# Interleaved steps of a hybrid attention and state-space block, set in the middle of projection units

## The chip, the cores and the metric

The kernel runs on one core of one Trainium2 chip. The metric is device microseconds per execution; the time shown is the median of three runs. The engines are TensorE (PE in the profile, with its weight loads as PEld), VectorE (DVE), ScalarE (ACT), GpSimd (POOL) and SyncE (SP), which issues the transfers.

## What is computed

One layer of a decoder trunk on 512 tokens of width 1024, in fp32: RMSNorm, one combined input projection, three branches that read it (A: banded attention over a window of 128 with sinks, B: dilated attention, C: a diagonal state-space model), each projected, gated and summed, an output projection, then a gated conv-FFN and a last RMSNorm. Cut to what the change touches:

```python
def banded_attention(q, k, v, max_offset, sink=None):   # 4 blocks of 128 queries
    ...                                                  # a block sees its own keys and the block before
    s = jnp.where(mask[None, :, None, None], s, NEG_INF)
    m = jnp.maximum(jnp.max(s, axis=-1, keepdims=True), sk)
    p = jnp.exp(s - m)
    l = jnp.sum(p, axis=-1, keepdims=True) + jnp.exp(sk - m)
    o = jnp.einsum("nbgrqk,nbkgd->nbgrqd", p, vv) / l

def s5_mixer(u, ...):                                    # 32 groups, 64 complex states each
    bu_re = jnp.einsum("bsgh,gph->bsgp", uf, bb_re)
    ...
    _, _, xr, xi = lax.associative_scan(combine, (a_re, a_im, bu_re, bu_im), axis=1)
    y = Re(C x) + D u

def hybrid_mixer(h, w_in, ...):
    proj = h @ w_in                                      # 1024 -> 5632 columns
    qa, ka, va, qd, kd, vd, u, g = jnp.split(proj, cuts, axis=-1)
    ...
```

## The kernel before

**Products.** fp32 products are made of three matmuls in a rounded format (fp32r): every weight is split into a high part `whi` and a low part `wlo`, the activations h likewise into `hTh` and `hTl`. `mm3` (L171 to L173) issues high by high, high by low, low by high. A weight chunk is loaded by SyncE into one of two `raw` buffers; `Chunk.split` then makes `whi` on ScalarE (L66) and `wlo` on VectorE (L92), or on VectorE (L91) and GpSimd in the start.

**Units.** The projections are a list of units. One unit makes 128 columns of the projection for all 512 tokens: `tile_mm` loops over 8 blocks of the contraction and issues three matmuls for each, 24 in all, into a PSUM bank of the tag "mm". ScalarE evicts it (`pj`, or `th` for a gate). Units 1 to 6 make q, k and v of branch A, 7 to 14 its gates, 15 to 24 q, k and v of branch B.

**Steps between units.** `run` goes through the units. For unit u it first splits a piece of the next chunk, then runs the functions that the table `plan` has for u (filled by `before(u, ...)`, L1347 ff.), then the unit itself. All engines take their instructions in the order in which this program issues them (a manual schedule), so the table is the order. The steps are:

- `attn_a(i)`, i = 0 to 3: branch A, block i, a generator of five stages (four for i = 0, which has one block of keys). Step 1: half of the scores into two "sc" banks (L764), maxima by VectorE (L771). Step 2: the other half, and then the whole softmax: maxima, `nmA`, `esA`, ScalarE's eight exponentials with sums (L780), `lA`, its reciprocal (L782), eight products (L269). Step 3: transposes of the probabilities into the "pt" banks (L794), copied to `pTA` by ScalarE. Steps 4 and 5: products with V into an "o" bank (L800), and for i > 0 the second block of keys.
- `ssm_m1(j)`, j = 0 to 3: 32 matmuls into two "sc" banks (L684), four products `z` by VectorE from these banks, sums by GpSimd, two scans by VectorE (L694, L695), then the products that make the states `X`, with differences by GpSimd.
- `ssm_m2(j)`: state to output, matmuls L718 and L720 into an "o" bank, four copies to `yS`, in turns ScalarE and VectorE (L725).
- `ssm_e(j)`: tables for `ssm_m1(j)`, on GpSimd. `ssm_ob(j)`: output matrices. `to_nat`: transposes of V.

**The start.** x is scaled by its norm in pieces (`scale1`: L363 for piece 0, L366 for piece 1), transposed by TensorE (`nt`, L340), converted to `hTh` and `hTl`, and the products for the state-space input u come first (`u_first`, L388).

Of the kernel before, what the change touches and what calls it, by code (L numbers as in the profile page):

```python
# [20 lines left out]
KD = DM // 128  # L21
# [10 lines left out]
def hybrid_block(  # L32
# [19 lines left out]
    def slot(shape, dt=F32, name="s"):  # L52
        return sl.tile(shape, dt, tag="s", name=name)
# [142 lines left out]

    def before(u, *fns):
        plan.setdefault(u, []).extend(fns)

    def run(first, live):  # L200
        order, start, last = [], [], {}
        for u, (c, _) in enumerate(units):
            if id(c) not in last:
                order.append(c)
                start.append(u)
            last[id(c)] = u
        state = {"loaded": 1, "live": live}
        done = [0] * len(order)
        done[0] = len(first.defs)

        def load_to(n):
            while state["loaded"] < min(n, len(order)):
                order[state["loaded"]].load()
                state["loaded"] += 1

        def split_to(ci, n):
            if ci >= len(order):
                return
            c = order[ci]
# [12 lines left out]
        for u, (c, fn) in enumerate(units):
            ci = order.index(c)
            cur = max(cur, ci)
            split_to(ci, 99)
            assert done[ci] == len(c.defs)
            fs = plan.get(u, []) + later
            later.clear()
            if u in AUX_FIRST:
                for f in fs:  # L240
                    f()
                fs = []
            if cur + 1 < len(order):
                left = len(order[cur + 1].defs) - done[cur + 1]
                split_to(cur + 1, done[cur + 1] - (-left // (start[cur + 1] - u)))
            for c2, n in early.get(u, []):
                split_to(order.index(c2), n)
            for f in fs:
                f()
            fn()  # L250
            if last[id(c)] == u and not c.own:
                state["live"] -= len(c.defs)

# [95 lines left out]
    vcol = cst([128, 8], "vcol")  # L349
# [7 lines left out]
    def rstd1(t):  # L357
        rstd_of(stat[:, 4 + t:5 + t], stat[:, t:t + 1])

    def scale1(t):  # L360
        xv, rs = xa[t // 2][:, t % 2, :], stat[:, 4 + t:5 + t]
        if t % 2 == 0:
            V.tensor_scalar(xv, xv, rs, None, op0=ALU.mult)  # L363
        else:
            copy_act(xv[:, 512:], xv[:, 512:], scale=rs)
            V.tensor_scalar(xv[:, :512], xv[:, :512], rs, None, op0=ALU.mult)  # L366
# [13 lines left out]
    def u_first(c):  # L380
        for a in range(2):
            ups[c, a] = bank("mm" if c == 0 else "o")
        half = KD // 2
        for kind, ks in ((0, range(KD)), (2, range(half)), (1, range(KD)), (2, range(half, KD))):
            for a in range(2):
                for k in ks:
                    w, xa_ = cu[c].get(k, a)[kind // 2], h_act(k)[kind % 2]
                    PE.matmul(ups[c, a][:, P0_], w, xa_[:, P0_], start=kind == 0 and k == 0,  # L388
                              stop=kind == 2 and k == KD - 1)
# [237 lines left out]
    def ssm_inj(j):  # L627
        bd = BDs[j % 2]
        INJ[j] = [slot([128, 4, 128], name="inj") for _ in range(2)]
        for i in range(2):  # L630
            pb = bank("pt")
            for t in range(4):
                PE.transpose(pb[:, t * 128:(t + 1) * 128],
                             bd[i][:, t].rearrange("p k g h -> p (k g h)"), ident)
            copy_act(INJ[j][i][:, :, :], pb[:, :].rearrange("p (t c) -> p t c", t=4))
        pk = bank("o", (128, 4, 32))
        for t in range(4):
            for i in range(2):
                PE.matmul(pk[:, t, :], bd[i][:, t].rearrange("p k g h -> p (k g h)"),
                          V0b[i][:, 4 * t + j].rearrange("p g h -> p (g h)"), start=(i == 0), stop=(i == 1))  # L640
        tz = TZ[j]
        for ti in range(4):
            for to in range(ti + 1, 4):
                b = 3 - (to - ti)
                copy_act(tz[32 * ti:32 * ti + 32, :, to, :], pk[32 * b:32 * b + 32, :, :])
        for ti in range(4):
            tt(tz[32 * ti:32 * ti + 32, :, ti, :], pk[96:128, :, :],
               DI[0][96:128].rearrange("p (t j) c -> p t j c", j=4)[:, :, j, :], ADD)
# [28 lines left out]
    def ssm_m1(j):  # L677
        Er, Ei = Es.pop(j)
        s = []
        inj = INJ.pop(j)  # L680
        for i in range(2):
            pb = bank("sc", (128, 4, 128))
            for t in range(4):
                PE.matmul(pb[:, t, :], inj[i][:, t, :], US[j][:, t, :], start=True, stop=True)  # L684
            s.append(pb[:, :, :].rearrange("p t c -> p (t c)"))
        a, b, zr, zi = (slot([128, 512], name="z")[:, :] for _ in range(4))
        tt(zr, s[0], Er, MUL)
        tt(a, s[1], Ei, MUL)
        tt(zi, s[1], Er, MUL)
        tt(b, s[0], Ei, MUL)  # L690
        tt(zr, zr, a, ADD, G)
        tt(zi, zi, b, SUB, G)
        a4 = A4s.pop(j)[:, :, :].rearrange("p t c -> p (t c)")
        V.tensor_tensor_scan(a, a4, zr, 0.0, op0=MUL, op1=ADD)  # L694
        V.tensor_tensor_scan(b, a4, zi, 0.0, op0=MUL, op1=ADD)  # L695
        X = [slot([128, 4, 128], name="X") for _ in range(2)]
        x3 = slot([128, 512], name="xt")[:, :]

        def sh(v):
            return v.rearrange("p (t c) -> p t c", c=128)[:, :, 0:127]  # L700

        for i in range(2):
            G.memset(X[i][:, :, 0:1], 0.0)
        tt(zr, a, Er, MUL)
        tt(x3, b, Ei, MUL)
        tt(X[0][:, :, 1:128], sh(zr), sh(x3), SUB, G)
        tt(zi, a, Ei, MUL)
        tt(b, b, Er, MUL)
        tt(X[1][:, :, 1:128], sh(zi), sh(b), ADD, G)
        Xs[j] = X  # L710

    def ssm_m2(j):
        if not yS:
# [26 lines left out]
    proj = {}  # L740
# [602 lines left out]
    def st_(g):  # L1343
        return lambda: next(g)
# [8 lines left out]
    before(4, lambda: ssm_inj(0), lambda: ssm_bd(1), lambda: ssm_e(0), st_(CP))  # L1353
    before(5, lambda: ssm_inj(1), lambda: ssm_bd(2))
    before(6, lambda: ssm_inj(2), lambda: ssm_bd(3), st_(CP))
    before(7, lambda: ssm_inj(3), st_(A[0]))
    before(8, lambda: VA.append(to_nat(proj["vA"], "VA")), lambda: ssm_ob(0), st_(A[0]))
    before(9, lambda: ssm_m1(0), lambda: ssm_ob(1), lambda: ssm_e(1))
    before(10, lambda: ssm_ob(2), st_(A[0]), st_(A[1]))
    before(11, lambda: ssm_ob(3), st_(A[0]), st_(A[1]))  # L1360
    before(12, lambda: ssm_m2(0), lambda: ssm_m1(1), lambda: ssm_e(2))
    before(13, st_(A[1]), st_(A[2]))
    before(14, st_(A[1]), st_(A[2]))
    before(15, st_(A[1]), lambda: ssm_m2(1), lambda: ssm_m1(2), lambda: ssm_e(3))
    before(16, st_(A[2]), st_(A[3]))
    before(17, st_(A[2]), st_(A[3]))
    before(18, st_(A[2]), lambda: ssm_m2(2), lambda: ssm_m1(3))
    before(19, st_(A[3]))
    before(20, st_(A[3]), lambda: VB.setdefault(0, [to_nat(proj["vB", 0], "VB0")]))
    before(21, st_(A[3]), lambda: VB[0].append(to_nat(proj["vB", 0], "VB1", True)), lambda: ssm_m2(3))  # L1370
    before(22, lambda: VB.setdefault(1, [to_nat(proj["vB", 1], "VB0")]))
    before(23, lambda: VB[1].append(to_nat(proj["vB", 1], "VB1", True)))
    for u, h in ((25, 0), (26, 0), (28, 0), (30, 0), (31, 1), (32, 1), (33, 0), (34, 1), (35, 0), (36, 0), (36, 1),
                 (37, 0), (38, 0), (39, 1), (41, 1), (42, 1), (43, 1), (44, 1)):
        before(u, st_(B[h]))
# [40 lines left out]
```

## Time and profile before

| what | value |
|---|---|
| median of three runs | 839.84 us (839.41 to 841.44) |
| the profiled execution | 840.54 us, of which 838.7 us span |
| TensorE busy | 814.7 us, 97% of the span |
| VectorE busy | 479.3 us, 57% |
| ScalarE busy | 353.8 us, 42% |
| GpSimd busy | 168.2 us, 20% |
| granted TensorE clock, mean | 0.994 of full speed |

Busy is the time in which an engine works on an instruction of its own; a matmul that waits inside a group of several is partly counted as busy. The rest of the 840.54 us lies around the span. A row of the waits says which instruction of an engine waited and which one released it.

### The profile page before, as it was taken

Reading aid. Unit: us, or ns where it says so; the run is one execution under the profiler, and the core shown is the slowest. Engines: PE = TensorE matmul, PEld = TensorE weight load, DVE = VectorE, ACT = ScalarE, POOL = GpSimd, SP = SyncE. Lnnn points to the kernel's source line nnn. Section 1 sums busy time; section 2 is a strip of 40 time slices with the busy share of each in tenths; the row PEclk is TensorE's granted clock in tenths of the full one; section 3 lists DMA queues with packets and bytes.
Section 4 is the critical chain, followed back from the end, with each engine's and each line's share of the span. In section 5 each row is a group of like instructions: output and inputs, shape, how many; then the busy total and the mean of one; then the engine's idle time right before and its main releaser. Section 6 shows DMA issues by size and latency. Waiting matters only on the chain.

```text
span 838.7 us, 10519 instructions
## 1 busy us (share of the span) xinstructions
PE 814.7 (97%) x4085; PEld 676.3 (81%) x4085; DVE 479.3 (57%) x921; ACT 353.8 (42%) x665; POOL 168.2 (20%) x217
## 2 busy tenths in 40 slices
PE   7999899989999999999999999999999999999996
PEld 7988768667777888888878998888888888888885
DVE  7898397697335637363655456556655555422313
ACT  5546453535435555352444344444444443313212
POOL 6199752562100100013530000000000000002002
PEclk9999999999999999999999999999999999999999
DMA  9333111111243113232362313333333323422402
GB/s 243 98 102 101 40 61 52 51 51 51 50 106 102 52 51 102 68 102 82 101 227 74 101 52 100 101 101 100 101 101 101 100 77 101 150 63 89 151 0 101
DMA packets 68278, 76.60 MB, mean 91 GB/s; under 512 B 8161, under 2 KB 55557, under 8 KB 68229
## 3 DMA queue, kind: packets, MB, share of 16 engines
q1 hardware_dynamic: 67972, 75.89, 28.4%
q8 instruction: 32, 0.52, 0.3%
q0 software_dynamic: 256, 0.05, 0.1%
q14 instruction: 18, 0.14, 0.1%
HBM read 73.81 MB, written 2.12 MB: 91 GB/s over the span
## 4 chain that ended last, share of the span: by engine, by line
PE 82%; DVE 9%; ACT 2%; issue 2%; POOL 2%; DMA 1%; SPq 0%; POOLq 0%; DVEq 0%; ACTq 0%
PE up L172 10%; PE up L173 10%; PE up L171 10%; PE mm L171 9%; PE mm L173 9%; PE mm L172 9%; PE acc L178 6%; PE acc L179 6%; PE acc L177 6%; DVE wlo L92 1%; DMA x<-in_x_dram 1%; DVE z L279 1%; PE sc L896 1%; PE nt L340 1%; POOL th L279 1%
## 5 line engine op out<-in xcount | busy, mean ns | idle before, releaser
L92 DVE TENSOR_TENSOR wlo<-raw,whi 128x1024 fp32r<-128x1024 f32 (+1 forms) x126 | 154.2, 1232 | 149.6 <-ACT whi L66 149.4
L66 ACT ACTIVATE whi<-raw 128x1024 fp32r<-128x1024 f32 (+1 forms) x126 | 127.4, 1024 | 58.4 <-PE acc L179 56.2
L171 PE MATMUL up<-hTh,whi 128*128 128x512 f32 (+1 forms) x384 | 142.9, 372 | 0.0
L172 PE MATMUL up<-hTl,whi 128*128 128x512 f32 (+1 forms) x384 | 142.8, 372 | 0.0
L173 PE MATMUL up<-hTh,wlo 128*128 128x512 f32 (+1 forms) x384 | 142.8, 372 | 0.0
L171 PE MATMUL mm<-hTh,whi 128*128 128x512 f32 (+1 forms) x336 | 132.3, 394 | 0.0
L173 PE MATMUL mm<-hTh,wlo 128*128 128x512 f32 (+1 forms) x336 | 129.5, 385 | 0.0
L172 PE MATMUL mm<-hTl,whi 128*128 128x512 f32 (+1 forms) x336 | 129.4, 385 | 0.0
L275 DVE SCALAR_TENSOR_TENSOR cc<-up,cpar,cc 128x511 f32<-128x511 f32 x88 | 66.0, 749 | 97.3 <-ACT cc L1108 95.7
L171 PEld LDWEIGHTS up<-hTh,whi 128*128 128x128 f32 x384 | 72.4, 189 | 12.5
L172 PEld LDWEIGHTS up<-hTl,whi 128*128 128x128 f32 x384 | 72.4, 189 | 12.4
L173 PEld LDWEIGHTS up<-hTh,wlo 128*128 128x128 f32 x384 | 72.4, 189 | 12.4
L171 PEld LDWEIGHTS mm<-hTh,whi 128*128 128x128 f32 x336 | 63.3, 188 | 14.5 <-issue 2.5
L173 PEld LDWEIGHTS mm<-hTh,wlo 128*128 128x128 f32 x336 | 63.2, 188 | 12.8
L172 PEld LDWEIGHTS mm<-hTl,whi 128*128 128x128 f32 x336 | 63.3, 188 | 11.5
L178 PE MATMUL acc<-wlo,gh 128*128 128x512 f32 x172 | 67.0, 390 | 0.0
L179 PE MATMUL acc<-whi,gl 128*128 128x512 f32 x172 | 67.0, 389 | 0.0
L177 PE MATMUL acc<-whi,gh 128*128 128x512 f32 x172 | 67.0, 389 | 0.0
L279 POOL TENSOR_TENSOR x<-x,gfin 128x512 f32<-128x512 f32 x4 | 5.2, 1289 | 296.8 <-ACT acc L1047 296.8
L1108 ACT ACTIVATE cc<-up,cpar 128x512 f32<-128x512 f32 x44 | 34.3, 779 | 61.2 <-PE up L173 60.5
L990 ACT ACTIVATE th<-mm 128x512 f32<-128x512 f32 x24 | 14.3, 594 | 71.1 <-PE mm L173 58.2
L66 ACT ACTIVATE gh<-cc 128x512 fp32r<-128x512 f32 x22 | 13.9, 632 | 59.4 <-DVE cc L279 59.4
(298 smaller groups left out, 1278.9 us busy)
## 6 DMA issues: line engine op xcount, KB each, us to landing
raw<-in_w_up_dram SPq DMA_DIRECT2D x22, 1024.0 KB, 5.0
raw<-in_w_in_dram SPq DMA_DIRECT2D x18, 1024.0 KB, 5.1
raw<-in_w_down_dram SPq DMA_DIRECT2D x10, 1024.0 KB, 5.0
x<-in_x_dram SPq DMA_DIRECT2D x8, 512.0 KB, 5.9
raw<-in_w_in_dram SPq DMA_DIRECT2D x8, 512.0 KB, 5.0
raw<-in_w_out_dram SPq DMA_DIRECT2D x4, 1024.0 KB, 5.1
raw<-in_w_branch_a_dram SPq DMA_DIRECT2D x4, 512.0 KB, 6.2
raw<-in_w_branch_c_dram SPq DMA_DIRECT2D x2, 1024.0 KB, 4.9
```

Of the source, the lines that this page charges most:

```text
L66: S.activation(o, i, AF.Copy)
L92: (lo_eng or V).tensor_tensor(view(lo), r, view(hi).bitcast(F32), op=ALU.subtract)
L171: PE.matmul(ps, wh, xh, start=first, stop=False)
L172: PE.matmul(ps, wh, xl, start=False, stop=False)
L173: PE.matmul(ps, wl, xh, start=False, stop=last)
L177: PE.matmul(ps, xh, wh, start=first, stop=False)
L178: PE.matmul(ps, xh, wl, start=False, stop=False)
L179: PE.matmul(ps, xl, wh, start=False, stop=last)
L275: emit(lambda: V.scalar_tensor_tensor(o, a, s, b, op0=op0, op1=op1))
L279: emit(lambda: (eng or V).tensor_tensor(o, a, b, op=op))
L990: S.activation(t, ps, AF.Tanh, scale=0.5)
L1108: S.activation(dst, ps, AF.Identity, bias=cpar[:, 3, f:f + 1], scale=cpar[:, 2, f:f + 1])
```

## The change

Four things are changed; what is computed stays.

1. `tile_mm` calls the functions in the list `midq` when half of its blocks are done, that is behind 12 of the 24 matmuls. `mid(u, ...)` puts functions there for unit u.
2. `ssm_m1` becomes a generator with two stages: up to the scans, and the rest.
3. The table of steps of units 7 to 24 is written anew, with `mid` for most of the scores and state-space steps.
4. In the start, `scale1(1)` and the copy of `vcol` come ahead of the split of the first weight piece.

```diff
     def tile_mm(ps, w, c, nk, act, o=slice(0, T)):
 
         for k in range(nk):
+            if k == nk // 2:
+                for f in midq:
+                    f()
+                midq.clear()
             xh, xl = act(k)
...
+            midq.extend(mids.get(u, []))
             fn()
...
         V.tensor_tensor_scan(a, a4, zr, 0.0, op0=MUL, op1=ADD)
         V.tensor_tensor_scan(b, a4, zi, 0.0, op0=MUL, op1=ADD)
+        yield
         X = [slot([128, 4, 128], name="X") for _ in range(2)]
...
     rstd1(1)
+    V.tensor_copy(vcol, pv[:, 0:8])
+    scale1(1)
     cu[0].split(0, V, G)
-    scale1(1)
-    V.tensor_copy(vcol, pv[:, 0:8])
     cu[0].split(1, V, G)
...
-    before(11, lambda: ssm_ob(3), st_(A[0]), st_(A[1]))
-    before(12, lambda: ssm_m2(0), lambda: ssm_m1(1), lambda: ssm_e(2))
-    before(13, st_(A[1]), st_(A[2]))
...
+    before(11, lambda: ssm_ob(3), st_(A[0]))
+    mid(11, st_(A[1]))
+    before(11, lambda: ssm_e(1))
+    before(12, lambda: ssm_m2(0))
+    mid(12, st_(A[1]))
+    before(13, st_(A[1]))
+    mid(13, st_(M[1]))
```

The whole table, with the unit at which each step is issued ("m" is the middle of the unit; A are the steps 1 to 5 of a block, M the two stages of `ssm_m1`, which before is one step):

| step | before | after |
|---|---|---|
| block 0: 1, 2, 3, 4 | 7, 8, 10, 11 | 7m, 8m, 10, 11 |
| block 1: 1 to 5 | 10, 11, 13, 14, 15 | 11m, 12m, 13, 14, 15 |
| block 2: 1 to 5 | 13, 14, 16, 17, 18 | 15m, 16m, 17, 18, 19 |
| block 3: 1 to 5 | 16, 17, 19, 20, 21 | 19m, 20m, 21, 22, 23 |
| `ssm_m1(0)` to `(3)` | 9, 12, 15, 18 | 9m 10m, 13m 14m, 17m 18m, 21m 22m |
| `ssm_m2(0)` to `(3)` | 12, 15, 18, 21 | 12, 15, 19, 24 |
| `ssm_e(1)`, `(2)`, `(3)` | 9, 12, 15 | 11, 16, 20m |

**TensorE between step 2 and step 3 of block 1.** Before, the scores stand at the start of unit 11 (its 24 matmuls are those of mm_1549), then come `ssm_m2(0)` (o_1583), the matmuls of `ssm_m1(1)`, all of unit 12 (mm_1645) and the transposes of the probabilities smA:

```order
L764 MATMUL sc_1516<-pj_1114,pj_933 128x256
L764 MATMUL sc_1517<-pj_1114,pj_933 128x256
...
L764 MATMUL sc_1517<-pj_1114,pj_1041 128x256
L171 MATMUL mm_1549<-hTh_125,whi_1354 128x512
...
L173 MATMUL mm_1549<-hTh_125,wlo_1435 128x512
L718 MATMUL o_1583<-us_903,tz_156 128x128
...
L684 MATMUL sc_1600<-us_978,inj_1047 128x128 x4
L684 MATMUL sc_1605<-us_978,inj_1048 128x128 x4
L171 MATMUL mm_1645<-hTh_125,whi_1354 128x512
...
L794 MATMUL pt_1677<-ident_83,smA_1471 128x128 x2
L794 MATMUL pt_1677<-ident_83,smA_1522 128x128 x2
```

Now they stand in the middle of unit 12, whose matmuls go to mm_1567:

```order
L777 MATMUL sc_1580<-pj_1114,pj_933 128x256
L777 MATMUL sc_1581<-pj_1114,pj_933 128x256
...
L777 MATMUL sc_1581<-pj_1114,pj_1041 128x256
L171 MATMUL mm_1567<-hTh_125,whi_1411 128x512
...
L173 MATMUL mm_1567<-hTh_125,wlo_1412 128x512
L807 MATMUL pt_1632<-ident_83,smA_1523 128x128 x2
L807 MATMUL pt_1632<-ident_83,smA_1586 128x128 x2
L807 MATMUL pt_1639<-ident_83,smA_1526 128x128 x2
```

The same scores and the same transposes, with 12 matmuls of a unit between them in place of 48 matmuls and two state-space steps.

**VectorE around the same softmax.** Before, the maxima (L771), sums and products of block 1, with the copies of yS behind them:

```order
L279 TENSOR_TENSOR ya1_1445<-o_1446,ya0_1444 128x4x128
L771 ISA smA_1522,mxA1_1461<-sc_1516,maskA_131 128x256
...
L771 ISA smA_1525,mxA1_1461<-sc_1517,maskA_131 128x256
L771 ISA mxA1_1461 128x1
L275 SCALAR_TENSOR_TENSOR nmA1_1462<-mxA1_1461,nsink_134 128x8
L279 TENSOR_TENSOR esA1_1464<-sink_123,nmA1_1462 128x8
L279 TENSOR_TENSOR lA1_1463<-lA1_1463,esA1_1464 128x8
L782 RECIPROCAL lA1_1463<-lA1_1463 128x8
L269 TENSOR_SCALAR smA_1471<-smA_1471,lA1_1463 128x256 x2
...
L725 COPY yS_1582<-o_1583 32x512 x2
L279 TENSOR_TENSOR z_1612<-sc_1600,E_1395 128x512
```

After:

```order
L92 TENSOR_TENSOR wlo_1544<-raw_1281,whi_1543 128x1024
L738 COPY yS_1549<-o_1550 32x512 x2
L784 ISA smA_1586,mxA1_1513<-sc_1580,maskA_131 128x256
...
L784 ISA smA_1589,mxA1_1513<-sc_1581,maskA_131 128x256
L784 ISA mxA1_1513 128x1
L286 SCALAR_TENSOR_TENSOR nmA1_1514<-mxA1_1513,nsink_134 128x8
L290 TENSOR_TENSOR esA1_1516<-sink_123,nmA1_1514 128x8
L290 TENSOR_TENSOR lA1_1515<-lA1_1515,esA1_1516 128x8
L795 RECIPROCAL lA1_1515<-lA1_1515 128x8
L280 TENSOR_SCALAR smA_1523<-smA_1523,lA1_1515 128x256 x2
...
L92 TENSOR_TENSOR wlo_1628<-raw_1415,whi_1627 128x1024
L290 TENSOR_TENSOR z_1671<-sc_1659,E_1488 128x512
```

The weight subtraction and the two copies of yS now stand ahead of the second four maxima; the next weight subtraction stands behind the products, as before, and the products z of `ssm_m1(1)` behind that.

**VectorE in the start.** Before:

```order
L330 TENSOR_SCALAR stat_127<-stat_127 128x1
L363 TENSOR_SCALAR x0_88<-x0_88,stat_127 128x1024
L330 TENSOR_SCALAR stat_127<-stat_127 128x1
L91 CAST whi_248<-raw_94 128x1024
L366 TENSOR_SCALAR x0_88<-x0_88,stat_127 128x512
L1257 COPY vcol_128<-o_237 128x8
L91 CAST whi_255<-raw_94 128x1024
```

After:

```order
L341 TENSOR_SCALAR stat_127<-stat_127 128x1
L374 TENSOR_SCALAR x0_88<-x0_88,stat_127 128x1024
L341 TENSOR_SCALAR stat_127<-stat_127 128x1
L1268 COPY vcol_128<-o_237 128x8
L377 TENSOR_SCALAR x0_88<-x0_88,stat_127 128x512
L91 CAST whi_251<-raw_94 128x1024
L91 CAST whi_255<-raw_94 128x1024
```

The scaling of the second half of x (L366, now L377) is ahead of the cast of the weight piece.

## Rows read from the trace of the kernel before

**Rows 1.** What TensorE waits for: line, releaser: us in total, times, longest.

```profile
PE nt L340 <- DVE x L366: 3.4, 1, 3.4
PE sc L684 <- DVE mxA L771: 3.3, 1, 3.3
PE sc L764 <- DVE mxA L771: 3.0, 2, 1.6
PE o L800 <- ACT pTA L66: 2.2, 2, 1.8
PE sc L764 <- DVE z L279: 2.1, 2, 1.6
```

**Rows 2.** TensorE's timeline: start, us, engine, line, operation, operands, [idle before <-releaser].

```profile
101.58 3.40 PE L684 MATMUL sc<-us,inj 128*128 128x128 f32 x16 [3.27 <-DVE mxA L771]
...
131.75 1.95 PE L684 MATMUL sc<-us,inj 128*128 128x128 f32 x16
...
183.43 1.82 PE L764 MATMUL sc<-pj 64*128 64x256 f32 x8 [1.45 <-DVE mxA L771]
...
152.16 1.14 PE L764 MATMUL sc<-pj 64*128 64x256 f32 x8
...
149.64 1.56 PE L800 MATMUL o<-pTA,VA 128*64 128x512 f32 x4 [1.80 <-ACT pTA L66]
...
158.93 1.08 PE L800 MATMUL o<-pTA,VA 128*64 128x512 f32 x4
```

**Rows 3.** Windows: busy us of PE, PEld, DVE, ACT, POOL, granted clock, DMA share, GB/s.

```profile
12.20:15.60 3.40, 3.40 (x18) 3.36 (x17) 2.99 (x8) 3.40 (x10) 2.02 (x1) 0.51 1.35 211
...
101.30:104.30 3.00, 2.71 (x12) 2.72 (x13) 0.99 (x10) 2.51 (x12) 0.00 (x0) 0.50 0.65 207
```

**Rows 4.** Timeline of the start: TensorE, VectorE and GpSimd.

```profile
13.23 3.32 PE L388 MATMUL mm<-hTh,whi 128*128 128x256 f32 x16
...
17.34 2.08 PE L388 MATMUL mm<-hTl,whi 128*128 128x256 f32 x16
...
8.46 2.63 DVE L366 TENSOR_SCALAR x<-x,stat 128x512 f32<-128x512 f32 x1
...
18.42 0.49 DVE L366 TENSOR_SCALAR x<-x,stat 128x512 f32<-128x512 f32 x1 [0.67 <-POOL stat L331]
...
7.53 0.90 POOL L331 TENSOR_TENSOR stat<-stat,mhalf 128x1 f32<-128x1 f32 x1 [0.93 <-DVE stat L330]
8.47 2.34 POOL L92 TENSOR_TENSOR wlo<-raw,whi 128x1024 fp32r<-128x1024 f32 x1
```

**Rows 5.** TensorE's timeline: the first and the last matmul of one unit (24 in all).

```profile
153.22 0.50 PE L171 MATMUL mm<-hTh,whi 128*128 128x512 f32 x1
...
158.61 0.39 PE L173 MATMUL mm<-hTh,wlo 128*128 128x512 f32 x1
```

**Rows 6.** The softmax of block 1, two rows of block 0's, and transposes that don't wait.

```profile
124.55 0.41 DVE L771 CUSTOM_DVE_ANT_0 smA<-sc,maskA 128x256 f32<-128x256 f32 x1
...
125.57 0.41 DVE L771 CUSTOM_DVE_ANT_0 smA<-sc,maskA 128x256 f32<-128x256 f32 x1
...
127.39 0.49 ACT L780 ACTIVATE smA<-smA,nmA 128x256 f32<-128x256 f32 x1
...
131.89 2.19 DVE L269 TENSOR_SCALAR smA<-smA,lA 128x256 f32<-128x256 f32 x8
...
101.66 0.29 DVE L771 CUSTOM_DVE_ANT_0 smA<-sc,maskA 128x128 f32<-128x128 f32 x1
...
102.50 0.39 ACT L780 ACTIVATE smA<-smA,nmA 128x128 f32<-128x128 f32 x1
...
151.13 1.09 PE L794 MATMUL pt<-ident,smA 128*128 128x128 f32 x8
```

**Rows 7.** A copy of yS on VectorE; the first exponential of block 3 on ScalarE.

```profile
135.25 1.05 DVE L725 COPY yS<-o 32x512 f32<-32x512 f32 x1
...
189.06 0.49 ACT L780 ACTIVATE smA<-smA,nmA 128x256 f32<-128x256 f32 x1
```

More of the change, by code (lines that the diff above doesn't have):

```diff
@@ L191, in hybrid_block @@
     plan = {}
+    mids = {}
+    midq = []
     def add(chunk, fn):
@@ L198, in before, with mid @@
         plan.setdefault(u, []).extend(fns)
+    def mid(u, *fns):
+        mids.setdefault(u, []).extend(fns)
     def run(first, live):
@@ L249, in run @@
                 f()
+            midq.extend(mids.get(u, []))
             fn()
+            assert not midq
             if last[id(c)] == u and not c.own:
@@ L382, in u_first @@
             ups[c, a] = bank("mm" if c == 0 else "o")
-        half = KD // 2
-        for kind, ks in ((0, range(KD)), (2, range(half)), (1, range(KD)), (2, range(half, KD))):
+        kh = KD // 2
+        for kind, ks in ((0, range(KD)), (2, range(kh)), (1, range(KD)), (2, range(kh, KD))):
             for a in range(2):
@@ L710, in ssm_m1 @@
         Xs[j] = X
+        yield
     def ssm_m2(j):
@@ L1355, in hybrid_block @@
     before(6, lambda: ssm_inj(2), lambda: ssm_bd(3), st_(CP))
[L1356 to L1359, printed above, removed]
-    before(11, lambda: ssm_ob(3), st_(A[0]), st_(A[1]))
-    before(12, lambda: ssm_m2(0), lambda: ssm_m1(1), lambda: ssm_e(2))
-    before(13, st_(A[1]), st_(A[2]))
-    before(14, st_(A[1]), st_(A[2]))
@@ L1364, in hybrid_block @@
[L1364 to L1371, printed above, removed]
@@ L1372, in hybrid_block @@
-    before(23, lambda: VB[1].append(to_nat(proj["vB", 1], "VB1", True)))
+    M = [ssm_m1(j) for j in range(4)]
+    before(7, lambda: ssm_inj(3))
+    mid(7, st_(A[0]))
+    before(8, lambda: VA.append(to_nat(proj["vA"], "VA")), lambda: ssm_ob(0))
+    mid(8, st_(A[0]))
+    before(9, lambda: ssm_ob(1))
+    mid(9, st_(M[0]))
+    before(10, lambda: ssm_ob(2), st_(A[0]))
+    mid(10, st_(M[0]))
+    before(11, lambda: ssm_ob(3), st_(A[0]))
+    mid(11, st_(A[1]))
+    before(11, lambda: ssm_e(1))
@@ new lines, in hybrid_block @@
+    before(12, lambda: ssm_m2(0))
+    mid(12, st_(A[1]))
+    before(13, st_(A[1]))
+    mid(13, st_(M[1]))
+    before(14, st_(A[1]))
+    mid(14, st_(M[1]))
+    before(15, st_(A[1]), lambda: ssm_m2(1))
+    mid(15, st_(A[2]))
+    before(16, lambda: ssm_e(2))
+    mid(16, st_(A[2]))
+    before(17, st_(A[2]))
+    mid(17, st_(M[2]))
+    before(18, st_(A[2]))
+    mid(18, st_(M[2]))
+    before(19, st_(A[2]), lambda: ssm_m2(2))
+    mid(19, st_(A[3]))
+    before(20, lambda: VB.setdefault(0, [to_nat(proj["vB", 0], "VB0")]))
@@ L1373, in hybrid_block @@
+    mid(20, st_(A[3]), lambda: ssm_e(3))
+    before(21, st_(A[3]), lambda: VB[0].append(to_nat(proj["vB", 0], "VB1", True)))
+    mid(21, st_(M[3]))
+    before(22, st_(A[3]), lambda: VB.setdefault(1, [to_nat(proj["vB", 1], "VB0")]))
+    mid(22, st_(M[3]))
+    before(23, st_(A[3]), lambda: VB[1].append(to_nat(proj["vB", 1], "VB1", True)))
+    before(24, lambda: ssm_m2(3))
     for u, h in ((25, 0), (26, 0), (28, 0), (30, 0), (31, 1), (32, 1), (33, 0), (34, 1), (35, 0), (36, 0), (36, 1),
```

## The prediction

> **What bounds the kernel now.** I read first the waits of TensorE, the engine that is hardly ever idle: all that it waits for is a dozen small items [rows 1]. One, of 3.4 us, lies in the start, where the transposes of x wait for VectorE to scale the second half of x. The others that count lie in units 7 to 24, where the attention and state-space steps are interleaved: 3.3 + 3.0 + 2.2 + 2.1 = 10.6 us, in seven pieces. Then the timeline of these places: a group of matmuls that starts after a wait is also longer than its twin that starts without one, because its later members wait inside the group, which the table of waits does not count. The first state-space group takes 3.40 us against 1.95, the second score group of a block 1.82 (the four that waited: 1.82, 1.64, 1.63, 1.82) against 1.14, a PV group 1.56 (two of them) against 1.08 [rows 2]. That is 1.45 + 2.35 + 0.96 = 4.8 us. So the interleaving costs TensorE 10.6 + 4.8 = **15.4 us** now, the most that a better order of these steps can give. Third, the granted clock: 0.51 for 3.4 us behind the wait at the start and 0.50 for 3.0 us behind the 3.27 us wait, which is the 1.2 GHz level after an idle stretch [rows 2, 3].
>
> **The start.** scale1(1) now stands ahead of the weight split on VectorE. Before, the second half of x is scaled from 8.46 on and takes 2.63 us, next to a 2.34 us weight subtraction of GpSimd that starts at the same time; the same operation on a later tile, alone, takes 0.49 [rows 4]. Now it starts as soon as GpSimd has the statistic (issued at 7.53, 0.90 long), between 8.1 and 8.5, and GpSimd's subtraction comes behind a cast that is behind it. So x is ready at 8.6 to 9.0, instead of 8.46 + 2.63 = 11.09: 2.1 to 2.5 us, and I take 2.5. The weight's cast comes half a microsecond or so later; its low half is wanted only by the second group of the product, several us behind, so that costs nothing. The idle time falls from 3.38 to about 1 us, so the clock should stay up: the first 16-matmul group of the product takes 3.32 us, one like it later 2.08 [rows 4]. ScalarE's conversions pace the first one too, so I take half of these 1.2, 0.6, bounds 0 and 1.2. Sum: **−3.1 us**, from −2.0 to −3.6. GpSimd's tables and the splits that follow stand behind these transposes, so I keep the gain whole.
>
> **What the interleaving removes.** Each unit's 24 matmuls are now cut in two halves of 12, and a step can stand in the cut; the scores of a block and the state-space groups no longer stand side by side. The waits of [rows 1] and the longer groups of [rows 2] come from one step that needs the score banks right behind another. With half a unit between them they go: a unit's matmuls run from 153.22 to 158.61 + 0.39 [rows 5], so half a unit is 2.8 us, and two banks are read in four maxima of 0.34 us spacing (124.55 to 125.57 for three [rows 6]), 1.4 us. I take all 15.4 as removed. Three small ones come back: an eviction on ScalarE at unit 9 that needs a buffer that GpSimd frees, block 0's transposes at unit 10, 1.5 units behind its scores, and VB's transposes near unit 24. No row isolates these; the nearest are the pieces of 2.2 / 2 and 2.1 / 2, 1.1 us each [rows 1]. I take 0.6 + 0.8 + 0.5 = **1.9 us**, from 0 to 3.3.
>
> **What it adds.** Here I expect the gain to go. In the old order the transposes of a block's probabilities (step 3) stand two units behind the scores that feed its softmax (step 2). In the new order that is 1.5 units for block 0 and **half a unit** for blocks 1, 2 and 3: step 2 in the middle of units 12, 16 and 20, step 3 ahead of units 13, 17 and 21. TensorE runs its list in order, so the whole softmax has to fit beside 12 matmuls. It does not. From the end of the last scores: four maxima, 1.4; from the last maximum's end to the first exponential 0.5 (in block 0 from 101.66 + 0.29 to 102.50); from the first exponential to the first product 4.5 (127.39 to 131.89, eight exponentials, sum and reciprocal); the products 2.19. That is 8.6 us [rows 6]. The transposes follow the products one by one, the last is done at 8.7; without a stall the group would be done at 2.8 + 1.09 = 3.9 (its twin at 151.13 [rows 6]). Stall: 4.8, say **4.7 us**, for blocks 2 and 3 each. For block 1 VectorE has two 1.05 us copies of yS [rows 7], of step m2(0) ahead of the unit, and a weight subtraction queued ahead of the maxima: 0 to 2.1 us more, I take 1.9, so 6.6. Behind the transposes on TensorE stands all of the next unit; behind the products on VectorE the next weight subtraction, wanted a unit later, which hides. Sum 6.6 + 4.7 + 4.7 = **16.0 us**.
>
> Each of them is an idle stretch of 3.5 us or more (from 2.8 behind the scores to the first product at 6.4), then a transpose every 0.27 us. The two idle stretches of that length in [rows 1] are followed by 3.0 and 3.4 us at half clock [rows 3], worth 1.5 to 1.7 each at most. But most of what comes right behind, the eight transposes, is paced by VectorE anyway and would lose nothing. From 0.35 to 1.5 each, I take 0.7: **2.0 us**.
>
> **Sum.** −3.1 − 15.4 + 1.9 + 16.0 + 2.0 = **+1.4 us**. Against the profiled execution, 840.54 us, that is 841.9; this execution lies 0.7 above the median of the runs, 839.84, so my time is **841.2 us**.
>
> **Rivals.** (a) Longer softmax chains: **slower**. In block 3 of the trace 3.81 us go from the end of the scores (183.43 + 1.82 [rows 2]) to the first exponential (189.06 [rows 7]), where my sum has 1.9; GpSimd was building its tables beside it, and a weight subtraction stood between the maxima. Tables 2 and 3 are issued in units 16 and 20 in the new order too, the units of these softmaxes, which speaks for it; that the block before it did not lose as much speaks against it (127.39 − 124.55 − 1.4 = 1.4 where mine has 0.5). Blocks 2 and 3 grow by 1.9 each: 841.2 + 3.8 = 845.0. It decides once the additions pass 1.2 us.
> (b) Smaller stalls: **faster**. The copies of yS are done before the scores come (they start with unit 12, 2.8 us ahead), the transposes keep the clock up, the start gives 3.6: 841.2 − 1.9 − 2.0 − 0.5 = 836.8. Nothing excludes the three together; the four copies of 1.05 behind m2's matmuls, more than 2.8 us on two engines, speak against the first.
> (c) The clock falls for three whole stretches of about 3 us behind the stalls, with unit matmuls in them: 3 × 1.5 = 4.5 instead of 2.0, **843.7**. The two places of [rows 3] speak for it, the pacing by VectorE against.
> The Trainium skill states it as a rule ("TensorE: Matmul & The Clock Gate", section "HAM oscillation — how this bites in real kernels"): an idle gap between bursts throttles the engine again each time, and the penalty is half of the throttled time. By that rule the time is that of (c); the two places at half clock agree with it, and the trace of before has no stall with slow transposes behind it that could tell (c) from my sum.
> (d) The gain at the start is absorbed, because the first weights and not x set the product's end: 841.2 + 3.1 = 844.3. Against: nothing but x is waited for there.
> (e) The stalls are 1.5 us shorter each, because the softmax takes 7.1 instead of 8.6 us: 841.2 − 4.5 = 836.7. For: my 8.6 is put together from pieces of two blocks; against: no block in the trace does it in less.
>
> **How the numbers follow.** About 0.3% (2.5 us) is what a measurement of this kernel can tell from no change, so "the same" is 837.3 to 842.4. Chances: my sum 0.46, (a) 0.19, (b) 0.11, (c) 0.09, (d) 0.06, (e) 0.09. The sum's own spread is about ±2 us (start, stalls and small waits by their bounds): of its 0.46 some 0.33 lie within "the same", 0.10 above, 0.03 below. Three quarters of (a), two thirds of (c) and all of (d) lie above: slower 0.10 + 0.14 + 0.06 + 0.06 = 0.36. Of (b) and (e) four fifths lie below: faster 0.03 + 0.16 = 0.19. The rest, 0.45, is the same. The range runs from (e), 836.7, leaving out the lower half of (b) and (e), to 846.5, leaving out the end of (a) with its clock: together no more than 0.2.
>
> **What would show it.** In the profile of the changed kernel the transposes of x start by 9.0 and run at full clock. The waits for maxima and for z are gone from the table of TensorE's waits, and one line for the transposes of P behind VectorE's products has three long pieces, 3.5 us or more each, the longest at block 1, with a clock near 0.5 behind them. Wrong would be: no such line, or pieces under 2 us (then the kernel is some 8 us faster, and my walk of the softmax fails), or scores that still wait for their banks.

## The result, and the profile after

The changed kernel takes 847.92 us (847.70 to 848.14, four runs) against 840.64 us of the kernel before beside it (839.41 to 841.51): a ratio of 1.0088, 95% interval 1.007 to 1.0105. It is **slower by 7.3 us**. The forecast was 841.2 us with a range up to 846.5, so the time lies outside the range.

The page of the changed kernel: the span grows from 838.7 to 845.9 us, TensorE is busy for longer, not for less, and the granted clock has two slices at 8 tenths that it did not have before.

```profile
span 845.9 us, 10521 instructions
...
PE 818.7 (97%) x4085; PEld 675.2 (80%) x4085; DVE 474.5 (56%) x921; ACT 355.2 (42%) x665; POOL 166.0 (20%) x217
...
PEclk9999999989899999999999999999999999999999
```

What TensorE waits for (instruction <- releaser: us in total, times, longest). The four lines of [rows 1] that stood for maxima, for z and for pTA are gone, and so is the 3.4 us wait at the start, of which 0.9 is left. One line stands in their place, and it is larger than the four together: the transposes of the probabilities wait for VectorE's products, three times, 13.0 us.

```profile
PE pt L807 <- DVE smA L280: 13.0, 3, 4.8
...
PE nt L351 <- DVE x L377: 0.9, 1, 0.9
...
PE pt L748 <- ACT pj L66: 0.7, 1, 0.7
...
PE mm L171 <- ACT th L1003: 0.4, 1, 0.4
```

The timeline at these three places (start, duration, engine, line, operands, [idle before <-releaser]); the groups of eight transposes last 2.2 us, where the unhindered one in [rows 6] lasts 1.09, because each transpose waits for its product. The VectorE rows are the first of the second four maxima of block 1 (behind a copy of yS) and of block 2 (which starts right at the scores' end, 166.37 + 1.13 = 167.50), and the eight products of block 2.

```profile
135.34 2.22 PE L807 MATMUL pt<-ident,smA 128*128 128x128 f32 x8 [4.77 <-DVE smA L280]
...
174.56 2.22 PE L807 MATMUL pt<-ident,smA 128*128 128x128 f32 x8 [4.11 <-DVE smA L280]
...
216.00 2.23 PE L807 MATMUL pt<-ident,smA 128*128 128x128 f32 x8 [4.10 <-DVE smA L280]
...
128.33 0.42 DVE L784 CUSTOM_DVE_ANT_0 smA<-sc,maskA 128x256 f32<-128x256 f32 x1
...
167.54 0.42 DVE L784 CUSTOM_DVE_ANT_0 smA<-sc,maskA 128x256 f32<-128x256 f32 x1 [0.51 <-PE sc L777]
...
174.06 2.19 DVE L280 TENSOR_SCALAR smA<-smA,lA 128x256 f32<-128x256 f32 x8
```

From 167.50 to the first product at 174.06 are 6.56 us and to the last one's end 8.75; the prediction had 6.4 and 8.6. The clock behind the stalls (window, busy us of PE, PEld, DVE, ACT, POOL, granted clock): the first two lines belong to block 1, then one each to blocks 2 and 3.

```profile
135.40:137.20 1.80, 1.80 (x8) 1.22 (x9) 1.80 (x8) 1.13 (x2) 0.00 (x0) 0.55 0.00 0
137.20:138.80 1.60, 1.60 (x6) 1.31 (x6) 0.96 (x1) 0.60 (x2) 0.00 (x0) 0.50 0.00 0
176.40:179.70 3.30, 3.30 (x10) 2.63 (x10) 0.98 (x1) 0.62 (x2) 0.00 (x0) 0.50 0.00 0
218.00:220.90 2.90, 2.90 (x10) 2.52 (x10) 1.29 (x3) 1.19 (x2) 0.00 (x0) 0.50 0.02 6
```

The clock is at its 1.2 GHz level while the transposes come one by one and then for another 1.6, 3.3 and 2.9 us, in which the next unit's matmuls run.

**The whole account.** The steps and units 7 to 24 go from the first instruction of unit 7 to the first scores of branch B:

```profile
85.17 0.72 PE L764 MATMUL sc<-pj 64*128 64x128 f32 x8
...
243.89 0.93 PE L858 MATMUL sc<-pj 64*128 64x128 f32 x8
```

```profile
84.51 0.48 PE L171 MATMUL mm<-hTh,whi 128*128 128x512 f32 x1
...
250.89 0.93 PE L871 MATMUL sc<-pj 64*128 64x128 f32 x8
```

The first two rows are of the kernel before, 158.72 us from one to the other; the next two of the changed kernel, 166.38 us. If the time from the start of each group of TensorE's rows to the start of the next is given to that group, less the waits, the stretch divides so:

| TensorE, units 7 to 24 | before | changed | difference |
|---|---|---|---|
| 432 matmuls of the units | 101.17 | 107.46 | +6.29 |
| scores, state-space groups and PV groups (L764, L684, L800 before) | 26.54 | 21.55 | −4.99 |
| transposes of the probabilities (L794) | 7.03 | 9.92 | +2.89 |
| other steps | 13.10 | 13.11 | 0.0 |
| waits | 10.88 | 14.34 | +3.46 |
| sum | 158.72 | 166.38 | +7.66 |

The changed kernel enters the stretch 0.66 us earlier (84.51 against 85.17) and leaves it 7.00 us later (250.89 against 243.89). So the order loses 7.7 us, and the start wins less than 1.

### The profile page after: what moved, and what is told of

It reads as the page before. It is cut to its first block, busy times and chain, and to the rows that moved or that the text cites. A ratio compares the mean times of both kernels' runs of the same rounds, so it can differ in the third digit from the quotient of the medians.

```text
span 845.9 us, 10521 instructions
## 1 busy us (share of the span) xinstructions
PE 818.7 (97%) x4085; PEld 675.2 (80%) x4085; DVE 474.5 (56%) x921; ACT 355.2 (42%) x665; POOL 166.0 (20%) x217
## 4 chain that ended last, share of the span: by engine, by line
PE 80%; POOL 8%; DVE 6%; ACT 3%; issue 2%; DMA 1%; SPq 0%; POOLq 0%; DVEq 0%; ACTq 0%
PE up L173 9%; PE up L172 9%; PE up L171 9%; PE mm L171 9%; PE mm L172 8%; PE mm L173 8%; PE acc L178 6%; PE acc L179 6%; PE acc L177 6%; POOL esc L290 1%; ACT smA L793 1%; PE pt L807 1%; POOL vt L290 1%; POOL t L290 1%; DMA x<-in_x_dram 1%
## 5 line engine op out<-in xcount | busy, mean ns | idle before, releaser
L92 DVE TENSOR_TENSOR wlo<-raw,whi 128x1024 fp32r<-128x1024 f32 (+1 forms) x126 | 151.8, 1213 | 146.2 <-ACT whi L66 146.1
L171 PE MATMUL mm<-hTh,whi 128*128 128x512 f32 (+1 forms) x336 | 135.1, 402 | 0.4 <-ACT th L1003 0.4
```

Source lines behind the costliest of these rows:

```text
L92: (lo_eng or V).tensor_tensor(view(lo), r, view(hi).bitcast(F32), op=ALU.subtract)
L171: PE.matmul(ps, wh, xh, start=first, stop=False)
```

## The experiments

Theory T1: the loss comes from the distance of half a unit between the scores and the transposes. Theory T2: the new order as such costs it, through its cut units. For the start, S1: VectorE's chain limits it; S2: TensorE's earlier transposes carry through.

**Step 3 half a unit later (e3_mid).**

```diff
-    before(13, st_(A[1]))
-    mid(13, st_(M[1]))
+    mid(13, st_(M[1]), st_(A[1]))
...                                   (the same for units 17 and 21)
```

> The changed kernel with step 3 of blocks 1, 2 and 3 half a unit later (middle of units 13, 17, 21, behind the state-space matmuls that stand there). Theory T1 (the softmax does not fit beside 12 matmuls; the three stalls, the transposes that follow at VectorE's pace and the half clock behind them cost 6.5, 6.7 and 6.2 us by the trace): 17 us faster than the changed kernel, about 830.5, the three long waits below 1 us each. Theory T2 (cutting the units and the new order as such cost the time): within 3 us of the changed kernel, 845 to 848.

Measured: 832.13 us (831.99 to 832.26), ratio to the kernel before 0.9893 (0.9878 to 0.9908). That is 15.8 us faster than the changed kernel and 8 us faster than the kernel before. TensorE's waits and the transposes of blocks 1 and 2:

```profile
PE o L733 <- POOL X L290: 1.8, 2, 0.9
...
PE mm L399 <- DVE whi L91: 1.3, 1, 1.3
...
PE pt L807 <- DVE smA L280: 0.3, 1, 0.3
```

```profile
135.44 2.07 PE L807 MATMUL pt<-ident,smA 128*128 128x128 f32 x8 [0.28 <-DVE smA L280]
...
170.67 1.85 PE L807 MATMUL pt<-ident,smA 128*128 128x128 f32 x8
...
235.25 0.93 PE L871 MATMUL sc<-pj 64*128 64x128 f32 x8
```

The 13.0 us line is down to 0.3. The transposes still follow VectorE (2.07 and 1.85 us against 1.09), but without an idle stretch ahead of them. The last row is the end of the stretch: 235.25, where the kernel before has 243.89 and the changed one 250.89. T1 stands, and T2 falls as the main cause: the same cut units with another distance make a kernel faster than the one before (what the cuts do cost, 2.1 us, comes below). The miss of 1.6 us against the expected 830.5 fits two waits for X behind GpSimd, 1.8 us, that the stalls had hidden, and what is left of the pacing.

**Between the two (e5_mid_first).** In the middle of units 13, 17 and 21 step 3 stands ahead of the state-space matmuls: 5.75 us behind the scores.

```diff
-    mid(13, st_(M[1]), st_(A[1]))
+    mid(13, st_(A[1]), st_(M[1]))
...                                   (the same for units 17 and 21)
```

> As e3_mid, but in the middle of units 13, 17 and 21 step 3 stands ahead of the state-space matmuls, so that it comes 5.75 us behind the end of the scores instead of 7.55. Theory T1 by the trace of the changed kernel (first product of the softmax 7.06 us behind the scores, the transposes then at VectorE's pace, 1.0 us longer than unhindered): waits of 1.3, 1.3 and 2 us, and 4 to 5 us slower than e3_mid, 836.5. Half clock no more, since the waits are under 2 us. If the position alone mattered and not the distance: like e3_mid, 832.

Measured: 837.35 us (836.57 to 837.51), ratio 0.9955 (0.9942 to 0.9968), 5.2 us slower than e3_mid.

```profile
PE pt L807 <- DVE smA L280: 4.3, 3, 2.1
```

The distance sets the loss: 847.9, 837.4 and 832.1 us at about 2.9, 5.75 and 7.55 us behind the scores. One part of the expectation was wrong: that waits this short leave the clock alone. Behind block 1's wait of 2.06 us and its slow transposes the state-space group takes 3.28 us, where the one of [rows 2] takes 1.95:

```profile
135.28 2.08 PE L807 MATMUL pt<-ident,smA 128*128 128x128 f32 x8 [2.06 <-DVE smA L280]
...
137.19 3.28 PE L695 MATMUL sc<-us,inj 128*128 128x128 f32 x16
```

```profile
135.30:137.20 1.90, 1.88 (x9) 1.09 (x10) 1.90 (x8) 1.17 (x2) 0.00 (x0) 1.00 0.00 0
137.20:140.40 3.20, 3.20 (x18) 3.20 (x18) 1.60 (x2) 0.60 (x1) 0.00 (x0) 0.56 0.01 3
174.40:176.40 2.00, 2.00 (x18) 1.99 (x18) 1.62 (x2) 0.60 (x1) 0.00 (x0) 1.00 0.00 0
```

The three windows are the transposes of block 1, the 3.2 us behind them, and the 2 us behind block 2's transposes (a wait of 1.39 us), where the clock stays. In block 1 the clock was still full at the end of the transposes, 4 us after the wait had begun at 133.22. The first stall of the changed kernel is like it: the clock was full through 4.7 us without a matmul, and fell once the transposes had begun (0.55 from 135.40 on, above).

```profile
130.60:135.30 4.70, 0.00 (x0) 0.00 (x0) 0.83 (x4) 4.68 (x18) 0.00 (x0) 1.00 0.00 0
```

In the changed kernel's blocks 2 and 3 it fell during the wait (0.57 from 173.00 to 174.00 and 0.55 from 214.00 to 215.00). So the fall came at different times after a wait began, and these runs do not tell how much of it is due to the wait and how much to the slow transposes; the same transposes behind a wait of 1.39 or 0.88 us did not bring it.

**Matmuls in the stalls (e4_warm).** The changed kernel, with 20, 17 and 17 matmuls ahead of step 3 that fill the wait; nothing uses what they write.

```diff
+    def warm_pe(n):
+        def f():
+            ps = bank("mm")
+            for k in range(n):
+                xh = h_act(k % KD)[0]
+                PE.matmul(ps[:, :], xh[:, 0:128], xh, start=True, stop=True)
+        return f
...
-    before(13, st_(A[1]))
+    before(13, warm_pe(20), st_(A[1]))
```

> The changed kernel with 20, 17 and 17 extra 128x512 matmuls in the three stalls, into a bank that the next unit but one overwrites (they compute nothing that is used; 0.23 us each, 4.6, 3.9 and 3.9 us of the stalls). Theory T1 with a clock share of 0.75 + 1.55 + 0.9 us read from the trace: 3.2 us faster than the changed kernel, about 844.7, with no half clock behind the stalls. If the clock behind the stalls costs nothing: 847.9. If it costs only the 2.0 us of the prediction: 845.9.

Measured: 843.59 us (842.65 to 844.35), ratio 1.003 (1.0021 to 1.004): 4.3 us faster than the changed kernel, with 54 matmuls more. Block 1's filling matmuls and transposes, and the windows over the transposes and the unit behind:

```profile
129.73 4.70 PE L1374 MATMUL mm<-hTh 128*128 128x512 f32 x20
...
134.69 2.08 PE L807 MATMUL pt<-ident,smA 128*128 128x128 f32 x8 [0.26 <-DVE smA L280]
```

```profile
134.60:136.60 2.00, 1.89 (x9) 1.14 (x9) 2.00 (x8) 1.28 (x2) 0.00 (x0) 1.00 0.00 0
136.50:139.40 2.90, 2.90 (x14) 2.41 (x15) 1.01 (x1) 0.60 (x1) 0.00 (x0) 1.00 0.00 0
```

The transposes take as long as before (2.08 us, VectorE's pace), but the clock is 1.00 behind them. So the three falls of the clock cost **4.3 us**, more than the 3.2 that I read from three gaps of the trace. The account says nearly the same: the unit matmuls take 107.46 us in the changed kernel, 103.49 in e4_warm and 103.29 in e3_mid, 4.0 and 4.2 less. The Trainium skill ("TensorE: Matmul & The Clock Gate", section "HAM oscillation — how this bites in real kernels") gives half of the throttled time as the penalty of each gap. Half of the 7.8 us (1.6 + 3.3 + 2.9) in which unit matmuls ran at the lower level is 3.9, so the trace agrees with it for these; counted over the transposes too, which VectorE paces at either level, it would give more than was measured.

**The start alone (e1_start), and the order alone (e2_order).**

```diff
+    V.tensor_copy(vcol, pv[:, 0:8])
+    scale1(1)
     cu[0].split(0, V, G)
-    scale1(1)
-    V.tensor_copy(vcol, pv[:, 0:8])
     cu[0].split(1, V, G)
```

> The kernel before with the change at the start alone. Theory S1 (VectorE's chain limits the start: in the changed kernel the first weight cast beside GpSimd's subtraction, 2.27 us, takes the place of the scaling that took 2.63, and VectorE's later pieces come only 0.6 us earlier): 0.6 to 0.7 us faster than before, 840.0. Theory S2 (the prediction's term; TensorE's earlier transposes carry through): 2.0 to 3.6 us faster, about 837.5.

> The changed kernel with the start of the kernel before, so that only the order of the steps is changed. Theory S1: the start was worth 0.5 to 0.8 us, so 848.4 to 848.8. Theory S2 (the prediction's 3.1 us, and an order that costs 4.5): 851.

Measured: the start alone 839.86 us (838.99 to 841.64), ratio 0.999 (0.998 to 1.000); the order alone 847.77 us (847.26 to 848.63), ratio 1.0096 (1.0079 to 1.0112). The two ratios of the order, 1.0096 without the start and 1.0088 with it, and the start's own 0.999 say 0.7 to 0.8 us for the start, with intervals that reach to nothing (the times alone say 0.5 and −0.15: the order alone ran at 847.77, below what either theory expected); not 3.1. Where the rest went is to be seen in the trace. The changed kernel, VectorE, GpSimd and TensorE:

```profile
8.00 0.49 DVE L377 TENSOR_SCALAR x<-x,stat 128x512 f32<-128x512 f32 x1 [0.38 <-POOL stat L342]
...
9.82 2.27 DVE L91 CAST whi<-raw 128x1024 fp32r<-128x1024 f32 x1 [0.73 <-DMA raw<-in_w_in_dram]
...
9.17 2.38 POOL L92 TENSOR_TENSOR wlo<-raw,whi 128x1024 fp32r<-128x1024 f32 x1 [1.20 <-DVE whi L91]
...
8.54 1.86 PE L351 MATMUL nt<-ident,x 128*128 128x128 f32 x15 [0.87 <-DVE x L377]
...
12.24 1.68 PE L399 MATMUL mm<-hTh,whi 128*128 128x256 f32 x12 [1.10 <-ACT hTh L354]
...
17.80 0.48 DVE L377 TENSOR_SCALAR x<-x,stat 128x512 f32<-128x512 f32 x1 [0.67 <-POOL stat L342]
...
56.97 0.66 PE L644 MATMUL pt<-ident,bd 128*128 128x128 f32 x4 [0.75 <-ACT bd L66]
```

The scaling takes 0.49 us and ends at 8.49, and the transposes start at 8.54, as predicted. But the second weight cast, which is 0.68 us in the kernel before, waits for its transfer until 9.82 and then stands beside GpSimd's subtraction: 2.27 us, to 12.09. The slow operation has only changed its place. TensorE's product waits for that cast (12.24; the profile names the last conversion, but e3_mid's table of waits names the cast at this place: `PE mm L399 <- DVE whi L91`), and VectorE comes to the last piece of x (L377) at 17.80, where the kernel before comes to it at 18.42 [rows 4]: 0.62 us. From there VectorE has one operation behind another until the tables for bd. Only in the kernel before does it wait in between for TensorE, 1.25 us for transposes of x; but GpSimd's next two subtractions, which run beside it until 25.07 and follow from VectorE's casts, hide that:

```profile
22.07 0.48 DVE L345 SCALAR_TENSOR_TENSOR hTl<-nt,vcol,hTh 128x256 fp32r<-128x256 f32 x1 [1.25 <-PE nt L340]
...
19.95 5.12 POOL L92 TENSOR_TENSOR wlo<-raw,whi 128x1024 fp32r<-128x1024 f32 x2 [1.57 <-DVE whi L91]
```

In five profiles the distance from this scaling to TensorE's first wait for bd is the same (and in the other two of these experiments, e3_mid and e6_start_casts, 39.20 and 39.19):

| kernel | scaling of the last piece of x | transposes of bd, behind a wait | distance |
|---|---|---|---|
| before | 18.42 | 57.59 | 39.17 |
| changed | 17.80 | 56.97 | 39.17 |
| e1_start | 16.84 | 56.04 | 39.20 |
| e5_mid_first | 17.62 | 56.82 | 39.20 |
| e7_mid_start | 17.40 | 56.62 | 39.22 |

So VectorE, with the subtractions that follow from its casts, sets the start in all of these kernels, whatever TensorE does there. In the profiled execution of e1_start the transfer landed earlier and VectorE won 1.6 us; the contention then met a copy of 16 x 128 elements, 1.26 us in place of 0.22:

```profile
8.39 1.43 DVE L91 CAST whi<-raw 128x1024 fp32r<-128x1024 f32 x2
...
13.25 1.26 DVE L1261 COPY prow<-lrow 16x128 f32<-16x128 f32 x1
...
16.84 0.49 DVE L366 TENSOR_SCALAR x<-x,stat 128x512 f32<-128x512 f32 x1 [0.67 <-POOL stat L331]
```

**Both casts ahead of the subtractions (e6_start_casts), and GpSimd held back (e7_mid_start).** e6_start_casts is e1_start with the two casts issued ahead of the two subtractions. e7_mid_start is e3_mid with that and a tiny copy on GpSimd that reads the second cast, so that GpSimd waits for it. The edit, shortened:

```diff
-    cu[0].split(0, V, G)
-    cu[0].split(1, V, G)
+    for i in range(2):
+        V.tensor_copy(hi[i], raw[i])
+    G.tensor_copy(gw, hi[1][:, 0, 0:1])        # in e7_mid_start alone
+    for i in range(2):
+        G.tensor_tensor(lo[i], raw[i], hi[i], op=ALU.subtract)
```

> The kernel before with the change at the start, and both weight casts on VectorE ahead of both subtractions on GpSimd, so that no cast stands beside a subtraction. Theory S1: the second cast falls from 2.27 to about 0.7 us, VectorE's chain comes 1.5 us earlier, 1.5 us faster than with the start change alone, about 838.5. Theory S2 (TensorE limits): no faster than the start change alone.

> e3_mid, with GpSimd's two first weight subtractions held back until both casts of VectorE are done (a tiny copy on GpSimd reads the second cast). Theory S1 (the time from VectorE's scaling of the last piece of x to the first wait for bd is a constant 39.2 us, whatever TensorE does): the second cast falls to 0.7 us, VectorE comes up to 1.5 us earlier, 1.0 to 1.5 us faster than e3_mid, 830.6 to 831.1. Rival: GpSimd's later subtractions delay the first product and the gain is 0 or below: 832.1 or more.

Measured: e6_start_casts 840.13 us (839.79 to 841.79), ratio 0.9995 (0.9985 to 1.0004); e7_mid_start 831.85 us (831.51 to 832.08), 0.3 us faster than e3_mid. e6_start_casts tells nothing on S1: GpSimd did not wait for the second cast, which came behind its transfer at 9.62 and took 2.54 us beside the subtraction. In e7_mid_start the cast is short, and the price is paid by the next operation that has GpSimd beside it:

```profile
9.35 0.69 DVE L1268 CAST whi<-raw 128x1024 fp32r<-128x1024 f32 x1 [0.21 <-DMA raw<-in_w_in_dram]
...
10.05 3.23 DVE L356 SCALAR_TENSOR_TENSOR hTl<-nt,vcol,hTh 128x256 fp32r<-128x256 f32 x8
...
13.31 1.76 DVE L1284 COPY prow<-lrow 16x128 f32<-16x128 f32 x1
...
10.24 4.74 POOL L1272 TENSOR_TENSOR wlo<-raw,whi 128x1024 fp32r<-128x1024 f32 x2
...
10.21 3.38 PE L399 MATMUL mm<-hTh,whi 128*128 128x256 f32 x16
...
17.40 0.49 DVE L377 TENSOR_SCALAR x<-x,stat 128x512 f32<-128x512 f32 x1 [0.67 <-POOL stat L342]
```

The 4.74 us of GpSimd's two subtractions now stand beside the copy of prow, 1.76 us in place of 0.22 in the kernel before. The eight conversions hTl beside them are not slowed. VectorE wins 0.5 us (17.40 against 17.87 in e3_mid), and the kernel 0.3, which the scatter of the runs (831.99 to 832.26 against 831.51 to 832.08) hardly tells from nothing. S1 stands by the distances, but my price for it (1.0 to 1.5) was wrong: moving the subtraction moves what it slows.

**What a switch costs (e8_cut, e9_uncut).** The account has the units' 432 matmuls at 103.29 us in e3_mid and 101.17 before, 2.1 us more with no half clock and no wait: 12 units are cut, 0.18 each. Two kernels put 24 extra transposes of the identity (unused) into the FFN's up units of the kernel before, in the middle of the unit or ahead of it. The line in which the two differ, shortened (− is e9_uncut, + is e8_cut):

```diff
             if 4 <= c < 10:
-                PE.transpose(bank("pt")[:, 0:128], ident, ident)
+                cutq.append(lambda: PE.transpose(bank("pt")[:, 0:128], ident, ident))
             tile_mm(fps[c, a, val], chunk, a, KD, h2_act, o)
```

> The kernel before with one extra 128x128 transpose of the identity (used by nothing) in the middle of 24 of the FFN's up units. Theory C (an interruption of a unit's matmuls costs about 0.2 us beside the step's own time, as the cut units of the changed kernel show, 5.81 us for 24 matmuls against 5.58): 24 x 0.3 = 7 us slower than the kernel before, 847.5. Rival: the transpose costs only its own 0.06 to 0.13 us: 842 to 843.5.

> The same 24 extra transposes, ahead of the same units. If an interruption in the middle costs more than one between units: faster than e8_cut by up to 5 us. If any switch costs the same: like e8_cut.

Measured: e8_cut 844.30 us (843.27 to 846.21), ratio 1.0043 (1.0031 to 1.0056); e9_uncut 845.19 us (843.64 to 845.53), ratio 1.0047 (1.0035 to 1.0059); the kernel before beside them 841.2. That is 3.1 and 4.0 us for 24 transposes, 0.13 and 0.17 each with the transpose itself. An interruption in the middle costs no more than one between two units, and my 0.3 was twice too high. So a cut is not dear as such; but each further change between a unit and a step costs a tenth or two of a microsecond, and the new order has twelve more of them. That this is the 2.1 us is an inference from the sizes; no run takes the cuts alone out of the new order. How much of the 0.13 to 0.17 is the switch and how much the transpose, these two runs do not tell.

**Further in the same direction (e10_later).** e7_mid_start with step 3 of blocks 1 and 2 ahead of units 14 and 18, step 4 in their middle, and `ssm_m2(1)` and `(2)` ahead of units 16 and 20.

```diff
-    mid(13, st_(M[1]), st_(A[1]))
-    mid(14, st_(M[1]))
-    before(15, st_(A[1]), lambda: ssm_m2(1))
+    mid(13, st_(M[1]))
+    mid(14, st_(M[1]), st_(A[1]))
+    before(15, st_(A[1]))
+    before(16, lambda: ssm_m2(1))
...                                   (the same for block 2, four units later)
```

> e7_mid_start, with step 3 of blocks 1 and 2 another half a unit later (ahead of units 14 and 18, step 4 in their middle) and ssm_m2(1) and (2) one unit later (16, 20). Theory T1: the rest of the stalls of e3_mid goes (0.28 + 1.0 us at block 1, 0.8 at block 2, two waits for X of 0.9 with 0.3 inside): 3 us faster, 829. Against it: the copies of yS then stand ahead of the maxima of blocks 2 and 3, as they do for block 1 now (0.65 us each), and block 3 keeps its distance of 7.55 us: 1.5 us faster, 830.3.

Measured: 828.92 us (828.16 to 829.97), ratio 0.9869 (0.9854 to 0.9883): the fastest of these kernels, 11 us faster than the kernel before. The waits for X are gone too. The only wait for products that is left is at block 3, whose step 3 did not move:

```profile
PE pt L807 <- DVE smA L280: 1.0, 1, 1.0
```

```profile
192.88 1.13 PE L777 MATMUL sc<-pj 64*128 64x256 f32 x8
...
195.94 0.42 DVE L784 CUSTOM_DVE_ANT_0 smA<-sc,maskA 128x256 f32<-128x256 f32 x1
```

It does not come from a shorter distance: from the scores' end (192.88 + 1.13 = 194.01) to TensorE's readiness for the transposes are 7.97 us, and in e3_mid, with 7.78, block 3 did not wait. Here the maxima start 1.9 us behind the scores, since the copies of yS of `ssm_m2(2)`, issued a unit later, and a weight subtraction now stand ahead of them on VectorE.

## Why the prediction was wrong, point by point

| term of the sum | predicted | measured on TensorE |
|---|---|---|
| start | −3.1 (−2.0 to −3.6) | −0.66 |
| waits and longer groups removed | −15.4 | −15.6 (10.6 of waits, 4.99 of groups) |
| small waits that come back | +1.9 (0 to 3.3) | +1.5 (0.42, 0.69 and 0.4 in block 0's transposes) |
| the three stalls | +16.0 | +15.5 (13.0 of waits, 2.5 of slow transposes) |
| clock behind the stalls | +2.0 (1.05 to 4.5) | +4.2 (4.3 by e4_warm) |
| more changes between units and steps | not in the sum | +2.1 |
| sum | +1.4 | +7.0 |

- **What held.** That all of the interleaving's old waits would go, that the softmax does not fit beside 12 matmuls, and the size of the stalls. By block the stalls were 4.77 + 1.0, 4.11 + 1.0 and 4.10 + 1.0, against 6.6, 4.7 and 4.7: the copies of yS in front of block 1 cost 0.7 and not 1.9 (its maxima start at 128.33, the scores end at 127.63), since the copies began as soon as the state-space outputs were there. The slow transposes count 1.0 each against groups of the same kernel that do not wait; against the groups of the kernel before they are the 2.5 of the table.
- **The start failed in the step "GpSimd's tables and the splits that follow stand behind these transposes, so I keep the gain whole".** VectorE's operations stand behind its own queue, not behind TensorE, and that queue won 0.6 us. I had priced the delay of the first cast at nothing ("half a microsecond or so later") and did not look at the second, which took 2.27 us beside the subtraction that had slowed the scaling. The 0.6 for the clock was not there to be won either: in e7_mid_start the first group of 16 matmuls takes 3.38 us at a granted clock of 1.00, and before it took 3.32, most of it at half clock, with ScalarE's eight conversions (3.02 us) beside it. Rival (d) had the absorption and its price (844.3), with another cause than the one that the runs showed.
- **The clock failed in the size,** though 4.2 lies within its own bounds. I took 0.7 a stall on the ground that the transposes are paced by VectorE anyway. They were, but the half clock lasted beyond them, 1.6 to 3.3 us into the unit. That is rival (c) (843.7), nearly whole.
- **A term was missing:** the price of the changes between units and steps, 2.1 us.
- **Rival (a) did not happen:** the first product of block 2 came 6.56 us behind the scores, as summed. The time lies near the one that (a) gave (845.0), for other reasons.
- **The range** treated the rivals as if only one could be true. (c) and (d) do not exclude each other; both held, and with the missing term they give 841.2 + 2.2 + 2.4 + 2.1 = 847.9. That this is the measured time to the tenth is luck: the other three terms take back 1.1 us (0.2 + 0.4 + 0.5), and the kernel before ran 0.8 us slower beside the changed one (840.64) than the 839.84 that the forecast started from.

## What to carry to other kernels

When a step is moved nearer to the one that feeds it, add up the whole chain between them on the other engines (here 8.6 us of maxima, exponentials and products) and compare it with the work that is left in between on the engine that must not wait; a move that frees one resource can be right and still be placed half a unit too early. An operation that is slow because another engine works beside it is not healed by moving it: look which operation will stand there next. And where two rivals can both be true, their prices belong into one bound together.

## What the runs showed of the hardware that was not expected

- The clock can fall late. In block 1 of the changed kernel it was 1.00 through 4.7 us without a matmul and 0.55 once the transposes had begun; in e5_mid_first it was 1.00 through a wait of 2.06 us and through eight transposes in 1.9 us, and 0.56 in the 3.2 us behind them. After waits of 1.39 and 0.88 us with the same slow transposes it did not fall.
- GpSimd's subtraction of 128 x 1024 elements (2.3 to 2.4 us) stretched several of VectorE's operations beside it: a scaling of 0.49 us to 2.63, a cast of 0.69 to 2.27 and 2.54, a copy of 0.22 to 1.26 and 1.76. Each of them ended shortly after the subtraction did (11.09 against 10.81 in the kernel before, 12.09 against 11.55 in the changed one, 15.07 against 14.98 in e7_mid_start), so they look held up until it was done. But not all are: the eight conversions hTl took 3.23 us beside it, 0.40 each, as one takes without it (25.10 to 25.50 in the changed kernel).
- Filling a stall with 54 useless matmuls made the kernel 4.3 us faster.
